# A scan's inputs, shifted through a scratch buffer in memory instead of 32 small on-chip transfers

## The chip, the core and the metric

The kernel runs on one core of a Trainium2 chip. TensorE (PE in the profile) multiplies, its weight loads are listed as PEld; VectorE (DVE), ScalarE (ACT) and GpSimd (POOL) do the rest; SyncE (SP) issues nearly all transfers, in its own order, one after the other. The metric is the device time of one execution in microseconds (us).

## The reference

One layer of an encoder trunk on 256 tokens of width 2048, in float32. A normalised input goes through one projection whose columns feed three groups, each normalised, joined and projected back; then an MLP of width 8192 follows.

```python
h = rmsnorm(x, norm_mix_pre[l])
proj = h @ w_in[l]
q_na, k_na, v_na, u_ssm, q_mem = jnp.split(proj, ...)
y_na = neighbourhood_attention(...)          # 8 heads of 128
y_ssm = s5_mixer(u_ssm, ...)                 # 32 groups of 16 channels, 64 complex states each, both directions
y_mem = memory_cross_attention(q_mem, ...)   # 4 heads, 256 memory tokens
y = jnp.concatenate([rmsnorm(y_na, ...), rmsnorm(y_ssm, ...), rmsnorm(y_mem, ...)], axis=-1)
x = x + rmsnorm(y @ w_out[l], norm_mix_post[l])
f = jnp.square(jax.nn.relu(rmsnorm(x, norm_mlp_pre[l]) @ w_ff1[l])) @ w_ff2[l]
x = x + rmsnorm(f, norm_mlp_post[l])
```

The `s5_mixer` is a linear recurrence over the tokens. Its input `u_ssm` (512 channels) is multiplied into the states (the increments), a scan runs over them forward and backward, and the states are multiplied out again.

## The kernel before

**Weights.** All weight matrices come as one stream of chunks of 128 x 1024 values (512 KB) in the order in which they are used (`plan`). `w_dma` issues chunk after chunk on SP into three raw buffers (`wraw`); a chunk may only be issued when VectorE has done with the chunk three before it. ACT copies a chunk into a rounded high part (`wh`), VectorE subtracts to get the low part (`wl`), and each product is three matmuls: high x high, high x low, low x high. `take(n)` hands the next n column blocks to TensorE; at the start of a chunk it has the chunk two ahead converted, and at its start and its middle it calls `tick`.

**Side work.** Everything that is not a weight matmul is a generator with a priority (a smaller number goes first), started by `spawn`. `tick` runs those that are due, by a planner's clock for each engine (`clk`, with costs written in the kernel); `after(ns)` lets that much of the planner's TensorE time go by, `until(f)` waits for a condition, and `drain` runs one to its end. The planner sets only the order in which instructions are written down for each engine. On the chip each engine takes its own list in order and waits at each instruction for what it needs.

**The scan.** The first 16 chunks give the mixer's input in `big`, and `g0_evac` writes it to `uT`: 128 partitions x 4 tiles (`ut`) x 256 tokens. The token order is such that a group's four consecutive tokens lie in four stretches of 64 columns. The increments want these four side by side in the partitions: `U4`, 128 x 16 x 64. 32 transfers of 16 partitions x 4 x 64 values move it there, all issued in a row on SP. `prep_b` makes the input weights of a tile in four power steps (`W`) on VectorE, has TensorE turn them, copies them to `W1T` and spawns `incr`, which multiplies them with `U4` as soon as `ssm_done` says that it is there by the plan, 6000 ns after the last issue. A tile has two increments (forward, backward) of 16 matmuls of 64 x 64; the profile lists each as two records. ACT puts the results in `XS`; `tree` scans two tiles at a time on VectorE (`ps`, `XS`), `ssm_out` multiplies out, and what follows prepares `yH`, `yL` for the gate's matmuls.

**The heads.** In the third stage (two groups of four heads) `att_task` does one head of the neighbourhood attention with priority 1, in six or so steps across the engines. `na_fin` then splits each head's result into `mixn`, high on ACT and low on VectorE, and the output projection's first group uses the heads in their order, two to a chunk.

The mixer's and the memory attention's stage lies around 60 to 130 us in the profile, the heads' after it to about 308 us, the output projection to about 425 us, the MLP behind that.

Of the kernel before, what the change touches and what calls it, by code (L numbers as in the profile page):

```python
# [11 lines left out]
F32 = mybir.dt.float32  # L12
# [19 lines left out]
NB = S // 4  # L32
# [11 lines left out]
SH_G = 500.0  # L44
BACK_V, BACK_G, BACK_A, BACK_TREE = 2600.0, 4000.0, 3000.0, 1700.0
WARM0, WARM1 = 7, 10
SUM_LAG = 5000.0
LAM_BACK = 900.0
GLU_AT = 2
# [55 lines left out]
def hybrid_kernel(ctx: ExitStack, tc: tile.TileContext, A: dict, out: bass.AP, dbg=None):  # L105
    nc = tc.nc
# [52 lines left out]
    V, G, ACT, PE = (Engine(e, r) for e, r in zip("VGAE", (nc.vector, nc.gpsimd, nc.scalar, nc.tensor)))  # L159
# [2 lines left out]
    wpool = ctx.enter_context(tc.tile_pool(name="wpool", bufs=3))  # L162
    small = ctx.enter_context(tc.tile_pool(name="small", bufs=4))
    ps = ctx.enter_context(tc.tile_pool(name="ps", bufs=1, space=PSUM))

    def acc():
        return ps.tile([128, 512], F32, name="acc", tag="bank", bufs=6)

    def att():
        return ps.tile([128, 512], F32, name="att", tag="bank", bufs=6)  # L170
# [4 lines left out]
    def tt(eng, o, a, b, op):  # L175
        eng.tensor_tensor(o, a, b, op=op)
# [10 lines left out]
    def act(o, i, f=AF.Copy, **kw):  # L187
        ACT.activation(o, i, f, **kw)
# [38 lines left out]
    def col(base, i=0):  # L227
        return vecs[:, base + i:base + i + 1]
# [7 lines left out]
    def spawn(gen, pri=1, uses="VA", after=None):  # L236
        i = sum(1 for t in tasks if t[0] <= pri)
        tasks.insert(i, [pri, gen, clk[after] + MARGIN + LAG[min(pri, 2)] if after else clk["E"], uses])
        return gen
# [37 lines left out]
    def after(ns):  # L277
        t = clk["E"] + ns
        while clk["E"] < t:
            yield  # L280

    def wait_for(g):
        while live(g):
            yield

    def done(e):

        t = clk[e] + MARGIN
        while clk["E"] < t:
            yield  # L290
# [152 lines left out]
    a2 = A2.enter_context(tc.tile_pool(name="a2", bufs=1, side="right"))  # L443
# [215 lines left out]
    uT = a2.tile([128, 4, 256], F32, name="uT")  # L659
    U4 = a2.tile([128, 16, NB], F32, name="U4")  # L660
# [9 lines left out]
    def prep_b(ut):  # L670
        yield from until(lambda: ut in loaded and clk["E"] > loaded[ut][1])
        raw = loaded[ut][0]

        wf = a2.tile([128, WROW], F32, name="W", tag="W", bufs=1)

        def power(l):
            a, n = (3 - l) * 16, WSTEP + (2 * l - 3) * 16
            return (wf[:, a:a + 2 * n].rearrange("p (d x) -> p d x", d=2)[:, :, 0:512]
                    .rearrange("p d (n l b) -> p d n l b", n=8, l=4)[:, :, :, 0, :])

        par = a2.tile([128, 4, 2, 2, 4], F32, name="par", tag="par", bufs=1)
        for i, x in enumerate((cfr, cfi, lbr, lbi)):
            act(par[:, i], x[:, 8 * ut:8 * ut + 8].rearrange("p (d q) -> p d q", d=2)[:, :, None, :]
                .to_broadcast([128, 2, 2, 4]))
        yield from done("A")
        for l in range(4):
            o = power(l)
            src = power(l - 1) if l else raw.rearrange("p (d n b) -> p d n b", d=2, n=8)
            r_, i_ = (par[:, 2 * min(l, 1) + i].rearrange("p d c q -> p d (c q)")[:, :, :, None]
                      .to_broadcast([128, 2, 8, 16]) for i in range(2))  # L690
            t = a2.tile([128, 2, 8, 16], F32, name="pt", tag="pt", bufs=1)
            tt(V, t, src, i_, mult)
            tt(V, o, src, r_, mult)
            tt(V, o[:, :, 0:4], o[:, :, 0:4], t[:, :, 4:8], sub)
            tt(V, o[:, :, 4:8], o[:, :, 4:8], t[:, :, 0:4], add)
            yield True
        yield from done("V")
        for d in range(2):
            act(W0[ut][:, d].rearrange("p c q j b -> p (c q) j b"),
                power(0)[:, d][:, :, None, :].to_broadcast([128, 8, 2, 16]))  # L700
        w0_done.add(ut)
        if ut % 2 == 0:
            XS[ut // 2] = a2.tile([128, 2, 16, NB], F32, name="XS", tag="AB", bufs=2)
        yield from done("A")
        for d in range(2):

            wt = a2.tile([128, 2, 4, 64], F32, name="W1T", tag="W1T", bufs=2)
            p = att()
            for n in range(8):
                for j in range(2):  # L710
                    h = slice(64 * j, 64 * j + 64)
                    PE.matmul(p[h, 64 * n:64 * n + 64], wf[h, WSTEP * d + 64 * n:WSTEP * d + 64 * n + 64], ident[h, h],
                              start=True, stop=True, skip_group_check=True, tile_position=(64 * j, 64 * j))
            act(wt.rearrange("p c q m -> p (c q m)"), p)
            spawn(incr(ut, d, wt, clk["A"] + MARGIN + LAG[2]), 2, "A")
            yield True
# [131 lines left out]
    ssm_done = []  # L848

    prepc, k0s, trees, out_done, w0_done, xs_part = (set() for _ in range(6))  # L850
    lam_done, pw_done, den_done = [], [], []

    def until(f):
        while not f():
            yield
# [125 lines left out]

    drain(rx)

    def g0_evac():
        b = st_rx["b"]
        for j in range(2):
            tt(V, qkm[:, 2 * j:2 * j + 2, 0, :], pq[j].rearrange("p (a b) -> p a b", a=2),
               b[:, None, :].to_broadcast([128, 2, 256]), mult)
        yield
        for u in range(4):  # L990
            tt(V, uT[:, u].rearrange("p (r c) -> p c r", c=16),
               pu[:, u * 256:(u + 1) * 256].rearrange("p (c r) -> p c r", c=16), b.rearrange("p (c r) -> p c r", c=16),
               mult)
        yield

        for q in range(4):
            for j in range(2):
                for i in range(4):
                    r = 64 * j + 16 * i
                    nc.sync.dma_start(U4[r:r + 16, q:16:4, :],  # L1000
                                      uT[32 * q + 16 * j:32 * q + 16 * j + 16, :, i * NB:(i + 1) * NB])
        yield from after(6000.0)
        ssm_done.append(1)
        if dbg:
            dbg("uT", uT.rearrange("p a b -> p (a b)"))
        yield
# [47 lines left out]
    def mem_task():  # L1054
        for h in range(MEMH):
            yield from att_task(qkm[:, h], vm[:, :, h * 128:(h + 1) * 128], None, (mixm[:, 0, h, :], mixm[:, 1, h, :]),
                                "mo", col(V_MO, h))
        yield from after(SUM_LAG)
        st_rx["mo"], _ = yield from rms([sums["mo"]], 1.0 / 512, "mo", bcast=False)
# [7 lines left out]
    def load_bias(h):  # L1067
        biasT[h] = a1.tile([128, 2, WIN_K], F32, name="bias", tag="xst", bufs=2)
        nc.sync.dma_start(biasT[h], A["bias"][h])

    for g in range(2):
        pv2 = [acc(), acc()]
        for k in range(KT):
            wh, wl = take(4)
            for t in range(2):
                s = slice(t * 128, (t + 1) * 128)
                mm_tok(pv2[t], xH[:, k, s], xL[:, k, s], wh, wl, start=(k == 0), stop=(k == KT - 1))
        vt = a1.tile([128, 2, 512], F32, name="v", tag="v", bufs=2)
        for t in range(2):
            act(vt[:, t, :], pv2[t], AF.Copy, scale=rsX[:, t:t + 1])  # L1080
        for h in range(4 * g, 4 * g + 4):
            load_bias(h)
            pp = acc()
            for j in range(2):
                for k in range(KT):

                    no_tree[0] = j == 1 and k >= KT - CH
                    wh, wl = take(1)
                    mm3(pp[:, j * 256:(j + 1) * 256], wh, wl, xH[:, k, :], xL[:, k, :], start=(k == 0),
                        stop=(k == KT - 1))  # L1090
            no_tree[0] = False
            qk = a1.tile([128, 2, 256], F32, name="qk", tag="qk", bufs=2)
            tt(V, qk, pp.rearrange("p (a b) -> p a b", a=2), rbX[:, None, :].to_broadcast([128, 2, 256]), mult)
            hh = h % 4
            naT.append(spawn(att_task(qk, vt[:, :, hh * 128:(hh + 1) * 128], biasT[h], yna[:, h, :], "na", None),
                             pri=1, after="V"))
    drain(mt)


# [11 lines left out]
    def na_rms():  # L1111
        yield from wait_for(nf)
        yield from after(SUM_LAG)
        st_rx["na"], _ = yield from rms([sums["na"]], 1.0 / 1024, "na", bcast=False)
# [130 lines left out]
    for t, c, _ in parts:  # L1245
        p = acc()
        s = slice(t * 128, (t + 1) * 128)
        b = slice(c.start - 1536, c.stop - 1536)
# [121 lines left out]
    def x1_task():  # L1370
        for o in range(4):
            for t in range(2):
# [8 lines left out]
    rt, r22, r24, vb, v, y, tn, r = (small.tile([128, 2], F32, name=n, bufs=1)  # L1381
                                 for n in ("rt2", "r22", "r24", "vb", "fv", "fy", "ft", "fr2"))
# [28 lines left out]
    for half in range(2):  # L1411
# [19 lines left out]
        for o in range(4):  # L1431
# [26 lines left out]
            if o < 3:  # L1458
                for t in range(2):
                    if half == 0:  # L1460
                        act(facc[:, t, c], po[t])
                    else:
                        tt(V, facc[:, t, c], po[t], facc[:, t, c], add)
                        q = cp.tile([128, 512], F32, name="ff", tag="ff", bufs=2)
# [88 lines left out]
```

## Time and profile before

| | |
|---|---|
| median of three runs | 1147.5 us (1146.65 to 1147.84) |
| profiled execution, its own time | 1145.56 us |
| its span, first to last instruction | 1143.8 us |
| instructions | 18188 |
| TensorE's mean granted clock | 0.991 |

In the profile's rows the first numbers are the start in us and the duration in us; then engine, line, operation, output tile and input tiles, shapes and count. In square brackets stands how long the engine was idle before and what ended that. Since every operation goes through one helper, nearly all rows carry its line, 156; tiles tell the groups apart. The row of a transfer on SP (`SPq`) is its issue, not its travel; "to landing" is from issue to the data's arrival. A row with x2 or more merges neighbours of one kind, and a matmul's modelled end overlaps the next one's start, so the distance of starts is the time that it takes.

### The profile page before, as it was taken

What the parts mean: (1) busy time and instruction counts of PE and PEld (TensorE: products, weight loads), DVE (VectorE), ACT (ScalarE), POOL (GpSimd) and SP (SyncE); (2) the same over time, 40 slices, a digit from 0 to 9 for tenths busy, and PEclk for the clock granted to TensorE, in tenths of its full rate; (3) what the DMA queues carried; (4) which work ended last, traced back from release to release, by engine and by line L of the source; (5) the groups of instructions that cost most, each with busy time, mean ns of one, the idle gap of its engine ahead of it and who ended that gap; (6) DMA issues with size and microseconds to landing.
All of it is one profiled execution on the core that took longest, in us unless ns stands there. A gap on an engine that the chain in (4) does not pass through costs nothing.

```text
span 1143.8 us, 18188 instructions
## 1 busy us (share of the span) xinstructions
PE 1113.1 (97%) x7144; PEld 962.5 (84%) x7144; DVE 717.4 (63%) x1068; ACT 563.6 (49%) x872; POOL 103.1 (9%) x171
## 2 busy tenths in 40 slices
PE   8996999999999999999999999999999999999996
PEld 8985889989977878888888888888888888888885
DVE  6783798899756766766665444445666665445454
ACT  6653665566564474544545434434544544344341
POOL 1760000020010061000000000000000000001010
PEclk9998999999999999999999999999999999999998
DMA  8873454445545665666666666666666665666673
GB/s 301 300 214 110 152 164 146 150 141 166 166 148 165 217 218 174 187 193 191 187 191 189 188 185 188 189 191 186 189 194 188 188 194 188 185 197 195 195 209 126
DMA packets 65287, 212.85 MB, mean 186 GB/s; under 512 B 9776, under 2 KB 12336, under 8 KB 65200
## 3 DMA queue, kind: packets, MB, share of 16 engines
q1 hardware_dynamic: 64912, 211.58, 60.5%
q8 instruction: 56, 0.92, 0.3%
q14 instruction: 31, 0.25, 0.1%
q10 hardware_dynamic: 288, 0.09, 0.0%
HBM read 209.02 MB, written 2.10 MB: 185 GB/s over the span
## 4 chain that ended last, share of the span: by engine, by line
PE 86%; DMA 3%; DVE 3%; POOL 3%; issue 2%; SPq 1%; ACT 1%; DVEq 0%; POOLq 0%; ACTq 0%
PE acc L156 77%; PE big L156 5%; PE att L156 5%; DMA wraw<-in_w_dram 3%; SPq L1000 1%; DVE wl L156 1%; ACT wh L156 1%; POOL u L156 1%; DVE W L156 0%; POOL cs L156 0%; POOL x L156 0%; DMA gpost<-in_post_dram 0%; POOL q L156 0%; POOL t L156 0%; POOL acc L156 0%
## 5 line engine op out<-in xcount | busy, mean ns | idle before, releaser
L156 DVE TENSOR_TENSOR wl<-wraw,wh 128x1024 fp32r<-128x1024 f32 (+1 forms) x372 | 458.9, 1235 | 378.7 <-ACT wh L156 378.3
L156 ACT ACTIVATE wh<-wraw 128x1024 fp32r<-128x1024 f32 (+1 forms) x372 | 391.5, 1054 | 456.4 <-PE acc L156 236.8
L156 PE MATMUL acc<-hs,wh 128*128 128x512 f32 (+1 forms) x996 | 346.0, 391 | 0.0
L156 PE MATMUL acc<-hs,wl 128*128 128x256 f32 x992 | 279.6, 282 | 0.0
L156 PEld LDWEIGHTS acc<-hs,wh 128*128 128x128 f32 x996 | 186.6, 188 | 38.4 <-ACT hs L156 0.2
L156 PEld LDWEIGHTS acc<-hs,wl 128*128 128x128 f32 x992 | 187.7, 189 | 0.0
L156 PE MATMUL acc<-wh,fH 128*128 128x512 f32 x448 | 178.9, 399 | 0.0
L156 PE MATMUL acc<-wh,fL 128*128 128x512 f32 x448 | 176.7, 394 | 0.0
L156 PE MATMUL acc<-wl,fH 128*128 128x512 f32 x448 | 175.7, 392 | 0.0
L156 PEld LDWEIGHTS acc<-wh,fL 128*128 128x128 f32 x448 | 84.1, 188 | 21.9
L156 PEld LDWEIGHTS acc<-wl,fH 128*128 128x128 f32 x448 | 84.2, 188 | 20.0
L156 PEld LDWEIGHTS acc<-wh,fH 128*128 128x128 f32 x448 | 84.1, 188 | 19.2
L156 PE MATMUL acc<-xH,wh 128*128 128x256 f32 x256 | 74.5, 291 | 0.0
L156 PE MATMUL acc<-xH,wl 128*128 128x256 f32 x256 | 71.9, 281 | 0.0
L156 PE MATMUL acc<-xL,wh 128*128 128x256 f32 x256 | 71.9, 281 | 0.0
L156 POOL TENSOR_TENSOR facc<-facc,g 128x512 f32<-128x512 f32 x6 | 9.6, 1622 | 476.5 <-DMA g<-in_g_dram 476.5
L156 PEld LDWEIGHTS acc<-xH,wh 128*128 128x128 f32 x256 | 48.4, 189 | 0.7
L156 PEld LDWEIGHTS acc<-xL,wh 128*128 128x128 f32 x256 | 48.4, 189 | 0.1
L156 PEld LDWEIGHTS acc<-xH,wl 128*128 128x128 f32 x256 | 48.3, 189 | 0.0
L156 PE MATMUL acc<-wh,mixn 128*128 128x512 f32 x128 | 41.5, 399 | 2.6 <-DVE half L156 1.4
L156 DVE TENSOR_TENSOR ps<-XS,pw 128x32 f32<-128x32 f32 (+9 forms) x44 | 30.3, 689 | 2.4 <-ACT XS L156 0.9
L156 PEld LDWEIGHTS acc<-wh,mixn 128*128 128x128 f32 x128 | 23.9, 188 | 8.8 <-DVE half L156 1.8
(303 smaller groups left out, 1452.1 us busy)
## 6 DMA issues: line engine op xcount, KB each, us to landing
wraw<-in_w_dram SPq DMA_DIRECT2D x369, 512.0 KB, 3.6
tokst<-in_xt_dram SPq DMA_DIRECT2D x4, 512.0 KB, 7.7
mst<-in_memT_dram SPq DMA_DIRECT2D x4, 512.0 KB, 5.0
tokst<-in_mt_dram SPq DMA_DIRECT2D x4, 512.0 KB, 5.9
x<-in_xt_dram SPq DMA_DIRECT2D x8, 256.0 KB, 5.6
out_dram<-facc SPq DMA_DIRECT2D x8, 256.0 KB, 2.5
xst<-in_xT_dram SPq DMA_DIRECT2D x7, 256.0 KB, 6.6
bias<-in_bias_dram SPq DMA_DIRECT2D x8, 160.0 KB, 3.8
```

The costliest lines, as they stand in the source:

```text
L156: return f(o, *a, **kw)
L1000: nc.sync.dma_start(U4[r:r + 16, q:16:4, :], uT[32 * q + 16 * j:32 * q + 16 * j + 16, :, i * NB:(i + 1) * NB])
```

## The change

The shift now goes through a scratch tensor `ud` in the chip's memory. Eight transfers write to it, each from 16 partitions, 64 KB in 256 pieces of 64 values; one transfer of 128 x 1024 values reads it back into `U4`. The eight are no longer issued in a row, but by a side task `shift` of priority 2, which lets 1300 ns of planned time pass after each. The increments are let in 14000 ns of planned time after the fetch is written down. Since turned weights wait longer for their use, `W1T` has four buffers, and a tile's weights are only turned when the tile two before it has its increments. The last two heads' attention gets priority 0.

```diff
+SHIFT_LAG = 14000.0
...
+    dram = ctx.enter_context(tc.tile_pool(name="dram", bufs=1, space=bass.MemoryType.DRAM))
...
         yield from done("A")
+        yield from until(lambda: ut < 2 or (ut - 2, 1) in xs_part)
         for d in range(2):
 
-            wt = a2.tile([128, 2, 4, 64], F32, name="W1T", tag="W1T", bufs=2)
+            wt = a2.tile([128, 2, 4, 64], F32, name="W1T", tag="W1T", bufs=4)
...
+    def shift():
+
+        ud = dram.tile([128, 16, NB], F32, name="ud")
+        for q in range(4):
+            for j in range(2):
+                r = 32 * q + 16 * j
+                nc.sync.dma_start(ud[64 * j:64 * j + 64, q:16:4, :].rearrange("(i b) u n -> b u i n", i=4),
+                                  uT[r:r + 16].rearrange("p u (i n) -> p u i n", i=4))
+                yield from after(1300.0)
+        nc.sync.dma_start(U4, ud)
+        yield from after(SHIFT_LAG)
+        ssm_done.append(1)
+
     def g0_evac():
...
-
-        for q in range(4):
-            for j in range(2):
-                for i in range(4):
-                    r = 64 * j + 16 * i
-                    nc.sync.dma_start(U4[r:r + 16, q:16:4, :],
-                                      uT[32 * q + 16 * j:32 * q + 16 * j + 16, :, i * NB:(i + 1) * NB])
-        yield from after(6000.0)
-        ssm_done.append(1)
+        spawn(shift(), 2, "V")
...
             naT.append(spawn(att_task(qk, vt[:, :, hh * 128:(hh + 1) * 128], biasT[h], yna[:, h, :], "na", None),
-                             pri=1, after="V"))
+                             pri=1 if h < 6 else 0, after="V"))
```

The SP queue in the memory attention's stage, before (`wraw` is a weight chunk, `U` the shifted input, `mst` and `Cw` other inputs):

```order
L459 DMA mst<-in_memT_dram 128x1024
L320 DMA wraw<-in_w_dram 128x1024
L1000 DMA U_112<-uT 16x4x64 x32
L320 DMA wraw<-in_w_dram 128x1024 x4
L741 DMA Cw<-in_c_dram 128x256
```

and after the change, whose lines are two or so further down:

```order
L461 DMA mst<-in_memT_dram 128x1024
L322 DMA wraw<-in_w_dram 128x1024 x2
L993 DMA ud<-uT 64x4x64
L322 DMA wraw<-in_w_dram 128x1024
...
L744 DMA Cw<-in_c_dram 128x256
L322 DMA wraw<-in_w_dram 128x1024 x3
L993 DMA ud<-uT 64x4x64
L322 DMA wraw<-in_w_dram 128x1024
...
L993 DMA ud<-uT 64x4x64
L322 DMA wraw<-in_w_dram 128x1024
L996 DMA U_114<-ud 128x1024
```

The 32 issues between two weight chunks are gone; eight stand singly, each behind one chunk, and the fetch one chunk behind the last of them.

TensorE at the first tile's increments, before, in the memory attention's stage (`memS` is its split input):

```order
L156 MATMUL acc<-memS,wh 128x256 x2
L156 MATMUL acc<-memS,wl 128x256
L156 MATMUL att<-U_112,W1T 64x64 x32
L156 MATMUL acc<-wh,memS 128x512
L156 MATMUL acc<-wl,memS 128x512
```

and after the change, ten of sixteen steps into the following matrix (`xH`, `xL` are the split main input):

```order
L157 MATMUL acc<-wl,xH 128x512
L157 MATMUL acc<-wh,xL 128x512
L157 MATMUL att<-U_114,W1T 64x64 x64
L157 MATMUL att<-CC,W_240 32x96 x16
L157 MATMUL acc<-wh,xH 128x512
```

The increments of the first two tiles now stand together, at the start of the fifth weight chunk behind the one with the fetch; the first tile's are 174 weight matmuls further back, the second's 42.

VectorE where the last heads are split, before (`wl` is a weight chunk's low part, `U` a step of the mixer's end):

```order
L156 SCALAR_TENSOR_TENSOR mixn<-yna,vecs,mixn 128x256
L156 TENSOR_TENSOR wl<-wraw,wh 128x1024 x2
L156 SCALAR_TENSOR_TENSOR mixn<-yna,vecs,mixn 128x256 x2
L156 TENSOR_TENSOR wl<-wraw,wh 128x1024
L156 SCALAR_TENSOR_TENSOR U_112<-gt,uT 128x16x16
L156 SCALAR_TENSOR_TENSOR mixn<-yna,vecs,mixn 128x256
```

and after the change:

```order
L157 TENSOR_TENSOR wl<-wraw,wh 128x1024 x2
L157 SCALAR_TENSOR_TENSOR mixn<-yna,vecs,mixn 128x256
L157 TENSOR_TENSOR wl<-wraw,wh 128x1024
L157 SCALAR_TENSOR_TENSOR U_114<-gt,uT 128x16x16
L157 TENSOR_TENSOR wl<-wraw,wh 128x1024
L157 SCALAR_TENSOR_TENSOR mixn<-yna,vecs,mixn 128x256
L157 MEMSET half 128x1
L157 TENSOR_TENSOR wl<-wraw,wh 128x1024
L157 SCALAR_TENSOR_TENSOR mixn<-yna,vecs,mixn 128x256
```

The first `mixn` row of the change is head 5's, then heads 6 and 7: head 5's has moved two weight splits forward, head 7's stays behind the same split, and the `U` step is no longer between that split and it.

## The prediction

> **What bounds the kernel now.** I read the page first (busy shares and the chain that ended last), then the busy time by stretches, and then the engines' own rows in the one stretch that stands out.
>
> ```profile
> PE 1113.1 (97%) x7144; PEld 962.5 (84%) x7144; DVE 717.4 (63%) x1068; ACT 563.6 (49%) x872; POOL 103.1 (9%) x171
> PE 86%; DMA 3%; DVE 3%; POOL 3%; issue 2%; SPq 1%; ACT 1%; DVEq 0%; POOLq 0%; ACTq 0%
> ```
>
> TensorE is busy for 97% of the span, and the chain runs through it for 86%. So a change that takes no matmul away can only win what TensorE loses, and the busy time by stretches says where that is. The columns are the stretch, its length, busy time of PE, weight loads, DVE, ACT and POOL, the granted TensorE clock, the DMA engines' share and GB/s:
>
> ```profile
> 68.00:88.50 20.50, 19.41 (x165) 17.55 (x165) 18.04 (x35) 10.77 (x21) 10.30 (x21) 0.92 0.55 160
> 88.50:103.40 14.90, 5.02 (x67) 4.16 (x65) 0.00 (x0) 0.32 (x1) 0.00 (x0) 0.67 0.31 84
> 103.40:130.00 26.60, 25.85 (x201) 22.23 (x200) 22.75 (x56) 18.71 (x27) 0.18 (x1) 0.99 0.53 168
> 130.00:200.00 70.00, 70.00 (x777) 64.26 (x777) 58.78 (x104) 41.99 (x90) 0.85 (x2) 1.00 0.49 150
> 250.00:308.00 58.00, 58.00 (x640) 56.62 (x642) 54.05 (x96) 35.94 (x71) 5.44 (x9) 1.00 0.59 175
> 308.00:345.00 37.00, 35.61 (x320) 28.95 (x309) 16.76 (x22) 22.32 (x41) 4.48 (x6) 1.00 0.47 140
> 345.00:400.00 55.00, 53.50 (x257) 43.88 (x256) 38.59 (x71) 25.02 (x35) 2.22 (x3) 1.00 0.62 191
> ```
>
> From 88.5 to 103.4 us TensorE works for 5.02 of 14.90 us, DVE and ACT for nothing or nearly so, at a clock of 0.67. Two later stretches lose 1.4 and 1.5 us; 130 to 200 and 250 to 308 lose none. The timeline of TensorE and of the SP queue shows the big loss:
>
> ```profile
> 88.49 0.28 PE L156 MATMUL acc<-memS,wl 128*128 128x256 f32 x1
> 88.70 0.44 PE L156 MATMUL att<-U,W1T 64*64 64x64 f32 x6
> 90.29 0.30 PE L156 MATMUL att<-U,W1T 64*64 64x64 f32 x2 [1.16 <-DMA U<-uT]
> ...
> 100.50 3.00 PE L156 MATMUL att<-U,W1T 64*64 64x64 f32 x50 [2.01 <-DMA U<-uT]
> 103.43 0.60 PE L156 MATMUL acc<-wh,memS 128*128 128x512 f32 x1
> ```
>
> ```profile
> 77.24 0.33 SPq L320 DMA_DIRECT2D wraw<-in_w_dram  x1
> 77.63 21.48 SPq L1000 DMA_DIRECT2D U<-uT  x32
> 99.22 6.54 SPq L320 DMA_DIRECT2D wraw<-in_w_dram  x4
> ```
>
> ```profile
> ACT wh L156 <- DMA wraw<-in_w_dram: 24.1, 5, 15.9
> ```
>
> The 32 shift transfers hold the SP queue for 21.48 us (0.67 us each). The first 64 increment records wait for them inside TensorE's order, and the weight chunks wait behind them: the last row, of the waits between 66 and 130 us, has ACT's copy waiting 15.9 us for one. Either wait alone would stop TensorE here, so both must go.
>
> **Part 1: the shift leaves the critical stretch.** From 88.70 to 103.43 TensorE spends 14.73 us on 64 increment records. The same work with its inputs there:
>
> ```profile
> 130.11 2.08 PE L156 MATMUL att<-U,W1T 64*64 64x64 f32 x64
> 132.12 0.91 PE L156 MATMUL att<-CC,W 128*32 128x96 f32 x32
> 79.34 0.40 PE L156 MATMUL acc<-memS,wh 128*128 128x256 f32 x2
> 82.16 0.40 PE L156 MATMUL acc<-memS,wh 128*128 128x256 f32 x2
> ```
>
> 132.12 - 130.11 = 2.01 us, so the stretch loses 14.73 - 2.01 = **12.72 us**. The last two rows start two neighbouring weight chunks: one chunk is 2.82 us of TensorE. It is 12 matmuls of 256 columns and 6 of 512, so 0.235 us for a wide one and 0.118 for a narrow one. In the changed order the increments of the first two tiles stand five chunks (14.1 us) behind the fetch of the shifted inputs, so they need it to land within that; the 2.01 us of each tile's matmuls is paid later and is already in the sum.
>
> What takes the place of the 32 issues? Eight, one behind each of eight weight chunks, and one fetch. Rows for what an issue costs and how a chunk and a shift transfer land:
>
> ```profile
> L1000 SPq DMA_DIRECT2D U<-uT x32: 585/593/970, 77.6 to 98.5; - x32
> DMA to landing us min/median/max: 1.8/1.9/5.3
> L320 SPq DMA_DIRECT2D wraw<-in_w_dram x372: 327/328/713, 1.2 to 1117.9; - x186
> DMA to landing us min/median/max: 2.5/3.6/8.8
> SPq L320 <- DVE wl L156: 29.9, 12, 4.7
> q1 hardware_dynamic: 1840, 0.38, 13.3%
> ```
>
> The trace has no issue of 256 pieces. From below it is a plain transfer's 0.33 us, from above four times the old one's 0.59 us for 64 pieces, 2.36 us; I take 0.97, the longest of the 32, since 128 pieces of a weight chunk cost no more than 0.33. Cover: a chunk comes every 2.82 us and its own issue takes 0.39 (77.24 to 77.63), so SP has 2.43 us per chunk, in which it now waits for VectorE (29.9 us in 12 waits between 66 and 136 us). Even 2.36 us fits under it, so I cost the eight at **0**; without that cover they would be 8 x 0.97 = 7.8 us. Queued behind each is only the next weight chunk, which ACT reads; its slack is what counts. For the DMA engines: between 84 and 99 us 1840 packets, nearly all of the old transfers, took 13.3% of 16 engines over 15 us, 31.9 us or 17.3 ns each. The outs move the same 2048 pieces: 35.5 us over 16 engines is 2.2 us, and the fetch is a chunk's worth, against a DMA share of 0.53. Also 0.
>
> [...] The pieces are 256 B and now go to memory, not to the on-chip buffer; no run so far shows such a write. [...]
>
> **Part 2: a wait that came with it.** After the burst of weight chunks VectorE is late once more:
>
> ```profile
> 104.17 1.23 DVE L156 TENSOR_TENSOR wl<-wraw,wh 128x1024 fp32r<-128x1024 f32 x1 [16.44 <-ACT wh L156]
> 113.52 0.56 PE L156 MATMUL acc<-memS,wh 128*128 128x256 f32 x2
> 114.83 0.38 PE L156 MATMUL acc<-memS,wl 128*128 128x256 f32 x1 [0.75 <-DVE wl L156]
> ```
>
> Two of these narrow matmuls take 0.24 us, so the third was due at 113.76 and lost 1.07. It comes from the split at 104.17 starting 0.74 us after TensorE resumed in mid-chunk (half a chunk is 1.41), that is 2.15 us into the chunk. Without the stall that split follows ACT's copy (1.06 us) at about 1.2 us, one us better. Bounds 0 and 1.07; I take **0.7**, as the power steps behind it stay in VectorE's list.
>
> **Part 3: the last heads.** In the first output group TensorE waits twice for attention heads:
>
> ```profile
> 341.83 0.40 PE L156 MATMUL acc<-wl,mixn 128*128 128x512 f32 x1
> 343.22 0.74 PE L156 MATMUL acc<-wh,mixn 128*128 128x512 f32 x2 [0.99 <-DVE mixn L156]
> 345.89 0.40 PE L156 MATMUL acc<-wl,mixn 128*128 128x512 f32 x1
> 347.65 0.73 PE L156 MATMUL acc<-wh,mixn 128*128 128x512 f32 x2 [1.36 <-DVE half L156]
> 344.47 1.06 ACT L156 ACTIVATE wh<-wraw 128x1024 fp32r<-128x1024 f32 x1 [1.85 <-PE acc L156]
> 345.56 1.23 DVE L156 TENSOR_TENSOR wl<-wraw,wh 128x1024 fp32r<-128x1024 f32 x1 [2.00 <-ACT wh L156]
> 346.70 0.58 DVE L156 SCALAR_TENSOR_TENSOR U<-gt,uT 128x256 f32<-128x256 f32 x1
> 347.13 0.46 DVE L156 SCALAR_TENSOR_TENSOR mixn<-yna,vecs,mixn 128x256 fp32r<-128x256 f32 x1
> ```
>
> At 0.235 us per matmul they were due at 342.07 and 346.12: 1.15 us are lost at head 5 and 1.53 at head 7. In the changed order head 5's low half stands two weight splits earlier, so its 1.15 goes. Head 7's keeps its place behind a weight split that can't start before TensorE has left the chunk before (ACT 344.47, DVE 345.56); only the `U` step ahead of it leaves, 347.13 - 346.70 = 0.43. So **1.58**, and 1.10 stays; bounds 0 (the heads are late elsewhere) and 2.68 (both go).
>
> **Part 4: the four buffers and the later scan.** Two more small buffers and one wait in the planner add no instruction. The scan over the increments starts four chunks later in VectorE's list: 4 x (2.82 - 1.22) = 6.4 us of it are pushed back. VectorE is idle for 11.2 us between 130 and 200, and for 3.95 between 250 and 308, which covers it if it spreads; the second scan ends behind the same weight split as before. Bounds 0 and 6.4; I allow **+0.6** for some wait.
>
> **Sum.** -12.72 - 0.7 - 1.58 + 0.6 = -14.4. The profiled execution took 1145.56 us (span 1143.8 and 1.76 around it), so a profiled one should take 1131.2; it lies 1.9 below the median shown, 1147.5, from which the predicted median is **1133.1 us**.
>
> **Rivals.** *A, slower: the SP queue becomes the stop.* If one of the eight issues holds SP for d us, the next chunk is late by d - 2.43, eight times. It eats the whole gain at d = 2.43 + 14.4/8 = 4.2 us; at 5 us it adds 20.6, 1153.7. For it: four times the pieces, four dimensions. Against it: nothing in the 32 rows goes above 0.97.
>
> *B: the way through memory is slow.* The fetch may only be issued when the last out has landed, and SP stands there with the next chunk behind it. The last out goes one chunk earlier, so beyond a landing of 2.82 + 2.43 - 0.33 = 4.9 us chunks are late. At the weights' worst, 8.8 us, that is 3.9 us: 1137.0. Against it: 1.9 us median for the old ones; for it: 5.3 as their worst. [...]
>
> *C: VectorE crowds.* If the 6.4 us fall where it has only 3.95 idle, TensorE waits 2.5 us for weight splits; if none is covered, 6.4. That is 1135 to 1139.5. For it: 54.05 of 58 us busy; against it: no TensorE loss there now.
>
> *D: the wait only moves*, to the increments' new place, because the fetch lands later than 14.1 us: then most of 12.72 comes back and the time is within 0.2% of 1147.5 or up to 1145.
>
> **How the numbers follow.** Forecast 0.72 (its own range 1130.5 to 1136), C 0.12, B 0.09, D 0.03, A 0.04. The low end is all upper bounds, 12.72 + 1.07 + 2.68 = 16.5, so 1131.0, less 0.5 for the spread of the runs; the high end is C's 1139.5, which holds B too. A measurement here can't tell less than 0.2% (2.3 us) from no change. Forecast, B and C are faster, and most of D: 0.94; same 0.02; slower is A, 0.04.
>
> **What would show it.** Right: no increment record waits for a transfer; the stretch from 88 us on shows TensorE busy and the clock at 1.00; SP's shift issues stand singly between weight chunks, under 2.4 us each; the matmul of head 5 follows without a wait, that of head 7 still waits about 1 us. Wrong: ACT's copies waiting for weight chunks between 80 and 120 us (A or B), weight matmuls waiting for VectorE's splits between 130 and 310 (C), increments waiting for the fetch (D).

## The result, and the profile after

| | before | after |
|---|---|---|
| median of 4 runs each (us) | 1147.08 (1146.43 to 1147.84) | 1131.14 (1130.65 to 1131.40) |
| profiled execution / its span (us) | 1145.56 / 1143.8 | 1131.40 / 1129.6 |
| mean granted TensorE clock | 0.991 | 0.996 |

The ratio is 0.986, 95% interval 0.9843 to 0.9877: 15.9 us less by the medians, 14.2 us less by the two profiled executions. 1133.1 us was predicted, with 1130.5 to 1139.5 as the range.

The page of the changed kernel, its busy shares and the chain that ended last:

```profile
PE 1109.0 (98%) x7144; PEld 958.8 (85%) x7144; DVE 716.3 (63%) x1068; ACT 563.7 (50%) x872; POOL 102.5 (9%) x171
PE 87%; DVE 4%; POOL 3%; DMA 2%; issue 2%; ACT 2%; SPq 0%; DVEq 0%; POOLq 0%; ACTq 0%
```

The SP queue is gone from the chain (0%, before 1%). Busy time by stretches in the changed kernel (stretch, its length, busy PE, weight loads, DVE, ACT, POOL, granted clock, DMA share, GB/s):

```profile
88.50:103.40 14.90, 14.64 (x95) 13.12 (x94) 13.87 (x39) 8.91 (x13) 0.00 (x0) 1.00 0.52 146
115.00:185.00 70.00, 70.00 (x804) 64.63 (x805) 52.72 (x94) 41.02 (x87) 0.18 (x1) 1.00 0.50 153
185.00:292.00 107.00, 105.10 (x1058) 98.15 (x1057) 96.52 (x157) 60.91 (x125) 12.01 (x16) 1.00 0.51 153
330.00:385.00 55.00, 53.69 (x258) 44.19 (x258) 39.43 (x72) 25.13 (x35) 2.22 (x3) 1.00 0.65 197
```

In the first of these stretches TensorE is now busy for 14.64 of 14.90 us at full clock (before: 5.02 us at 0.67). In the third it loses 1.90 us, where the kernel before lost nothing. The SP queue's timeline shows what stands in place of the 21.48 us of issues, and the groups of the scratch tile what an out costs:

```profile
79.08 0.69 SPq L993 DMA_DIRECT2D ud<-uT  x1
82.81 0.33 SPq L322 DMA_DIRECT2D wraw<-in_w_dram  x1
83.19 0.59 SPq L993 DMA_DIRECT2D ud<-uT  x1
...
112.84 0.33 SPq L322 DMA_DIRECT2D wraw<-in_w_dram  x1
113.83 0.33 SPq L996 DMA_DIRECT2D U<-ud  x1
```

```profile
L993 SPq DMA_DIRECT2D ud<-uT x8: 581/586/1172, 79.1 to 110.2; - x8
L996 SPq DMA_DIRECT2D U<-ud x1: 331/331/331, 113.8 to 113.8; - x1
DMA to landing us min/median/max: 3.6/4.6/6.1
```

The outs stand singly between weight chunks, 0.59 us each (median), and land after 3.6 us or more (median 4.5; the last row also counts the fetch). TensorE's timeline after the change, with the first increments, all that it still waits for between 75 and 400 us, and the rows just ahead of two of these waits:

```profile
98.09 0.40 PE L157 MATMUL acc<-memS,wh 128*128 128x256 f32 x2
98.75 0.38 PE L157 MATMUL acc<-memS,wl 128*128 128x256 f32 x1 [0.26 <-DVE wl L157]
...
125.70 3.95 PE L157 MATMUL att<-U,W1T 64*64 64x64 f32 x128
...
204.89 0.50 PE L157 MATMUL acc<-wl,xH 128*128 128x512 f32 x1 [0.44 <-DVE wl L157]
215.35 1.97 PE L157 MATMUL att<-XS,CC 128*32 128x63 f32 x128 [0.56 <-DVE XS L157]
240.74 0.38 PE L157 MATMUL acc<-xH,wl 128*128 128x256 f32 x1 [0.90 <-DVE Cw L157]
...
332.87 0.39 PE L157 MATMUL acc<-wl,mixn 128*128 128x512 f32 x1
334.57 0.73 PE L157 MATMUL acc<-wh,mixn 128*128 128x512 f32 x2 [1.31 <-DVE mixn L157]
```

The 128 increment records of the first two tiles run without a wait. What is left is VectorE: a wait of 0.26 us where the kernel before had one of 0.75 (at 114.83), three new waits of 1.90 us together between 200 and 245, and 1.31 at head 7. Head 5's wait is gone. ACT's copies still wait for weight chunks between 80 and 120 us, 6.5 us in four waits, the longest 1.9; none of that reaches TensorE.

A wait in brackets counts from the modelled end of the matmul before, and so shows less than is lost: by the distance of starts, the prediction's measure, the 0.26 are 98.75 - (98.09 + 0.24) = 0.42 us (before: 1.07) and the 1.31 are 334.57 - (332.87 + 0.235) = 1.47 us (before: 1.53). Both measures are used below, each under its name.

### The profile page after: what moved, and what is told of

Its sections match the earlier page's. It is cut to its first block, busy times and chain, and to the rows that moved or that the text cites. A ratio compares the mean times of both kernels' runs of the same rounds, so it can differ in the third digit from the quotient of the medians.

```text
span 1129.6 us, 18148 instructions
## 1 busy us (share of the span) xinstructions
PE 1109.0 (98%) x7144; PEld 958.8 (85%) x7144; DVE 716.3 (63%) x1068; ACT 563.7 (50%) x872; POOL 102.5 (9%) x171
## 3 DMA queue, kind: packets, MB, share of 16 engines
q1 hardware_dynamic: 64672, 212.10, 62.1%
## 4 chain that ended last, share of the span: by engine, by line
PE 87%; DVE 4%; POOL 3%; DMA 2%; issue 2%; ACT 2%; SPq 0%; DVEq 0%; POOLq 0%; ACTq 0%
PE acc L157 78%; PE big L157 5%; PE att L157 5%; DMA wraw<-in_w_dram 2%; DVE wl L157 2%; ACT wh L157 1%; POOL u L157 1%; DVE W L157 0%; POOL t L157 0%; POOL cs L157 0%; POOL x L157 0%; POOL q L157 0%; DVE pt L157 0%; DVE XS L157 0%; POOL k L157 0%
## 5 line engine op out<-in xcount | busy, mean ns | idle before, releaser
L157 ACT ACTIVATE P<-P,mn 128x160 f32<-128x160 f32 (+1 forms) x24 | 10.8, 449 | 43.9 <-DVE mn L157 43.9
```

The lines of the kernel that those rows point to most:

```text
L157: return f(o, *a, **kw)
```

## Experiments

Each ratio is against the kernel before, run on the same chip beside it (median there 1146.59 us for the first four experiments, 1147.20 for the next four, 1147.06 for the last two). The scheduler makes its lists anew for every edit, so for each experiment it is said whose VectorE list it has: where two kernels have the same list, row for row, they differ in the transfers, the increments' place and a few rows of ACT around them alone. No run takes the four buffers or the wait in the planner away by itself. In the code cuts, lines in brackets or in plain words are notes, and the making of a scratch tensor is left out.

### 1. The heads alone

```diff
 (kernel before)
-                             pri=1, after="V"))
+                             pri=1 if h < 6 else 0, after="V"))
```

> The kernel before with one edit: the last two attention heads run in the scheduler's first class. My theory: the wait of TensorE for head 5 (1.15 us) goes and that for head 7 falls from 1.53 to 1.10 us, so the time is 1.58 us shorter than before, about 1145.5 us, and the loss from 88.5 to 103.4 us stays whole. Rival: the heads' order costs nothing or is worth nothing by itself, because the wait of head 7 takes over what head 5 gives up: within 0.3 us of before. In the changed kernel the first output group waits 1.31 us for head 7 and not for head 5, so by it I expect 1.15 + 0.2 = 1.4 us.

Measured: 1143.64 us, ratio 0.9973 (0.9963 to 0.9983), 2.95 us less. That is more than either expectation (1.58 and 1.4 us); by the interval it is 1.9 to 4.2. Its stretch around the last heads, columns as above:

```profile
330.00:385.00 55.00, 55.00 (x400) 45.90 (x400) 35.26 (x57) 28.44 (x41) 3.55 (x6) 1.00 0.58 172
```

TensorE loses nothing there (before: 2.35 us of waits, 2.68 by starts). In this list head 7's mixing, too, stands one weight split earlier; in the list of the changed kernel, with the same head order, it does not. So the wait of head 7 that I read off the changed order belongs to that order, not to the head edit.

### 2. The burst kept, the increments late

```diff
 (changed kernel: lag, guard, four buffers, head order)
 def shift():
+    32 transfers U4[r:r+16, q:16:4, :] <- uT[...], as before, in one burst
-    eight outs to ud, one per after(1300.0); then U4 <- ud
     yield from after(SHIFT_LAG)
```

> The changed kernel's lag, guard, four buffers and head order, but the shift itself as before: 32 on-chip transfers issued in one burst, no scratch in memory. The increments stand later in TensorE's order, so they no longer wait; the weight chunks still queue behind 21.5 us of issues. My theory (either wait alone stops TensorE): the chunk that is issued at 99.2 us lands, is copied and split by about 103.9, while TensorE runs out of split weights at 90.1 (half a chunk behind 88.7) or, with one more chunk ready, 92.9 us; 11.0 to 13.8 us are lost in place of 12.72, and with the heads' 1.4 the time is 1143 to 1147 us. Rival (the increments' wait was the loss and the weights would have come in time): most of 12.7 us is won, about 1133 us.

Measured: 1148.49 us, ratio 1.0016 (1.0008 to 1.0025): nothing is won, and the 1143 to 1147 us expected are missed. The timelines of the SP queue and of TensorE in this run, and the stretch behind the wait, columns as above:

```profile
80.77 21.54 SPq L992 DMA_DIRECT2D U<-uT  x32
102.41 1.48 SPq L321 DMA_DIRECT2D wraw<-in_w_dram  x3
```

```profile
107.55 0.80 PE L157 MATMUL acc<-memS,wh 128*128 128x256 f32 x2 [11.24 <-ACT wh L157]
108.81 0.58 PE L157 MATMUL acc<-memS,wl 128*128 128x256 f32 x1 [0.46 <-DVE wl L157]
```

```profile
103.40:115.00 11.60, 6.99 (x77) 6.36 (x78) 7.05 (x22) 4.57 (x7) 0.00 (x0) 0.53 0.68 216
```

No increment waits for a transfer any more, and TensorE stands still for 11.24 + 0.46 = 11.70 us all the same, now for a weight chunk. So the weights' wait alone is enough, as the prediction had it (11.0 to 13.8 expected). The other half, that the increments' wait would be enough with the weights in time, has no run. The stop cost more than its length here: the granted clock behind it was 0.53, so that the 6.99 us of busy time hold another 3.3 us of loss, an estimate from these two numbers (6.99 x 0.47; before, the clock from 103.4 to 130 us was 0.99). This is one reason why the time is not below that of before, as expected; the other is shared by the next run.

### 3. The outs in a row

```diff
 (changed kernel)
                 nc.sync.dma_start(ud[...], uT[...])
-                yield from after(1300.0)
         nc.sync.dma_start(U4, ud)
```

> The changed kernel with its eight outs and the fetch issued in a row behind one weight chunk, not spaced; the increments then stand about five chunks earlier in TensorE's order. My theory: SP is held 8 x 0.59 + 4.5 (landing of the last out) + 0.33 = 9.5 us, the next weight chunk is 7.1 us late; from the kernel before, 5.3 to 8.1 us of that are slack of the weights on their way to TensorE, so 0 to 1.8 us are lost between 80 and 100 us, and the earlier scan takes away some of the 1.9 us of waits between 200 and 250 us: 1129.5 to 1133 us. Rival (the bound of 4.9 us that I used for a wait on SP): 9.5 - 4.9 = 4.6 us lost, about 1135.7 us. Rival (the stretch has far more slack): nothing lost, 1129.5 us or less.

Measured: 1136.77 us, ratio 0.9911 (0.9897 to 0.9924). My range, 1129.5 to 1133, is missed. The number is near that of the first rival, but the profile is not that rival's. The SP queue's timeline, and then TensorE's waits for VectorE, all that it has between 75 and 345 us:

```profile
80.45 6.09 SPq L993 DMA_DIRECT2D ud<-uT  x8
88.67 0.35 SPq L995 DMA_DIRECT2D U<-ud  x1
89.07 1.37 SPq L322 DMA_DIRECT2D wraw<-in_w_dram  x3
```

```profile
248.42 0.39 PE L157 MATMUL acc<-xH,wl 128*128 128x256 f32 x1 [0.70 <-DVE wl L157]
252.29 0.39 PE L157 MATMUL acc<-xH,wl 128*128 128x256 f32 x1 [0.80 <-DVE wl L157]
268.95 0.39 PE L157 MATMUL acc<-xH,wl 128*128 128x256 f32 x1 [0.24 <-DVE wl L157]
282.87 0.81 PE L157 MATMUL att<-qk 128*128 128x160 f32 x4 [0.93 <-DVE qk L157]
...
334.85 0.74 PE L157 MATMUL acc<-wh,mixn 128*128 128x512 f32 x2 [0.94 <-DVE mixn L157]
338.86 0.74 PE L157 MATMUL acc<-wh,mixn 128*128 128x512 f32 x2 [0.94 <-DVE mixn L157]
```

SP is held from 80.45 to 89.02 us, 8.57 us, and TensorE does not wait once between 75 and 248 us. The weights have that much slack. Runs 2 and 3 size it. In the changed kernel the chunk behind the first out goes out 3.73 us after it (82.81 - 79.08). By that measure the next chunk went out 17.9 us late in run 2 (102.41 - 80.77 - 3.73), and TensorE waited 11.7, so some 6.2 us are slack, an estimate from this one execution; in run 3 it was 4.9 us late (89.07 - 80.45 - 3.73), which is less. The two runs have the same VectorE list, and even the same order on TensorE and ACT; only the transfers differ. Their medians differ by 1148.49 - 1136.77 = 11.72 us and their profiled executions by 14.09, where run 2's wait and clock make 11.70 + 3.3 = 15.0 us and a pause of 1.34 us in run 3's profile (see run 10) works the other way. That the medians' 11.72 equals the wait alone is chance: run 2's times spread over 3.9 us.

What run 3 loses, it loses between 248 and 340 us, six waits for VectorE of 4.55 us in all, and so does run 2. Run 3's increments:

```profile
97.34 2.08 PE L157 MATMUL att<-U,W1T 64*64 64x64 f32 x64
```

They come 28 us earlier than in the changed kernel (125.70), the scan follows them, and VectorE's list meets TensorE's worse; that the earlier scan is the reason is not shown.

### 4. The 32 transfers on chip, spread

```diff
 (changed kernel; no scratch)
+    32 transfers U4[r:r+16, q:16:4, :] <- uT[...], as before,
+    behind two of every three: yield from after(700.0)
-    eight outs to ud, one per after(1300.0); then U4 <- ud
-SHIFT_LAG = 14000.0
+SHIFT_LAG = 6000.0
```

> The shift as before, 32 on-chip transfers without a scratch in memory, but spread over about 15 weight chunks, one to three behind each; lag 6000, guard, four buffers and head order as in the changed kernel. My theory (what counts is that no weight chunk queues behind more than the 2.43 us that SP has left per chunk): three issues of 0.6 to 0.7 us are at most 2.0 us and stay hidden, the time is 1131 us, up to 1.5 us more since the increments come half a chunk or more later than in the changed kernel. Rival (fewer and larger transfers by way of memory are what helps): the 32 issues cost part of their 21.5 us again, 1135 us or more.

Measured: 1128.35 us, ratio 0.9833 (0.9819 to 0.9847), 2.8 us under the changed kernel. The old transfers work as well as the new ones once they are spread; one to three issues between chunks cost TensorE nothing here, where from 75 to 395 us it waits only once, 0.26 us for VectorE. But this kernel's list differs from the changed one's too:

```profile
135.88 3.95 PE L157 MATMUL att<-U,W1T 64*64 64x64 f32 x128
```

The increments come 10 us later than there, so the 2.8 us may be the transfers' or the list's. Run 7 separates that.

### 5 and 6. The old lists, with the shift moved

```diff
 (changed kernel)
                 nc.sync.dma_start(ud[...], uT[...])
-                yield from after(1300.0)
+                if j == 1:
+                    yield from after(1300.0)
 (run 5 only)
-                             pri=1 if h < 6 else 0, after="V"))
+                             pri=1, after="V"))
```

With two outs behind each of four chunks VectorE's list comes out, row for row, as in the kernel before (run 5) and as in run 1 (run 6).

> The changed kernel without the head order and with its eight outs issued two behind each of four weight chunks: by this VectorE's list is the same, row for row, as in the kernel before, and only the shift and the first 64 increments have moved. My theory (the stall of 12.72 us and VectorE's lateness behind it, 0.81, are all that the move takes away): 13.5 us shorter than before, about 1133.3 us, ratio 0.988, with the waits for heads 5 and 7 still there and no new wait between 190 and 310 us. Rival (moving the increments costs something by itself): those waits come with it, 1135 us or more.

> The same with the head order: VectorE's list is then, row for row, that of the run with the heads alone. My theory (the two parts add up, and what the changed kernel gives back between 200 and 340 us comes from the planner's new list and not from the shift): the 2.95 us of the heads and the 13.5 of the move, 16.5 together, about 1130.2 us, no wait of TensorE between 105 and 395 us. Rival (moved increments and early heads get into each other's way whatever the list is): the 1.9 us of waits between 200 and 245 us and the 1.3 us at head 7 are there again, 1132 us or more.

Measured: run 5 1130.70 us, ratio 0.9861 (0.9847 to 0.9874), 16.5 us less than before; run 6 1126.55 us, ratio 0.9821 (0.9808 to 0.9835), 20.65 us less. Run 6 beats both kernels. The stretches of run 6, columns as above, and then TensorE's waits for heads in run 5:

```profile
185.00:292.00 107.00, 107.00 (x1093) 100.49 (x1095) 96.17 (x152) 61.89 (x125) 14.44 (x18) 1.00 0.52 160
292.00:330.00 38.00, 38.00 (x440) 31.58 (x429) 20.46 (x27) 23.19 (x42) 4.59 (x6) 1.00 0.48 144
330.00:385.00 55.00, 55.00 (x265) 45.54 (x264) 38.22 (x69) 27.30 (x39) 4.54 (x5) 1.00 0.67 211
```

```profile
328.21 0.73 PE L157 MATMUL acc<-wh,mixn 128*128 128x512 f32 x2 [0.99 <-DVE mixn L157]
332.63 0.73 PE L157 MATMUL acc<-wh,mixn 128*128 128x512 f32 x2 [1.35 <-DVE half L157]
```

Run 6 has TensorE busy without a gap from 185 to 385 us; run 5 has the two waits for heads of before, 0.99 and 1.35 us, and none between 190 and 310. Run 5's gain of 16.5 us (14.5 to 17.6 by the interval) is above the 13.5 expected; the two profiled executions differ by 15.6. The starts of the same matmuls tell where: run 5 is 0.79 us ahead of the kernel before at 73.26 us (74.05 there), 14.65 ahead at 117.47 (132.12), so 13.9 us belong to the moved shift, near the 13.5; the sections on run 10 and on the clock show where differences of the other kind come from. Moving the shift brings no wait of its own, then, and the head order is worth what it was worth alone (4.15 us by these medians, 2.64 by the two profiled executions, 2.95 in run 1). Run 6 is 3.7 us below the 1130.2 expected, for the same reason: it gains 15.0 us on run 1 between 73.47 and 117.29 us (73.83 and 132.68 there), since run 1's stall is a longer one, and run 1 has a pause besides (see run 10). The changed kernel has both edits and misses 4.6 us of run 6. Between the two lie the list and the pairing of the outs, and run 7 shows that the way by memory costs nothing against the one on chip.

### 7. The changed kernel, a longer lag

```diff
-SHIFT_LAG = 14000.0
+SHIFT_LAG = 20000.0
```

> The changed kernel with a lag of 20000 in place of 14000: VectorE's list is then, row for row, that of the run with 32 spread on-chip transfers, and the two differ only in how the inputs are shifted, eight outs and a fetch by way of memory or 32 transfers on chip. My theory (the way of the transfers costs nothing as long as no chunk queues behind them): the same time as that run, 1128.4 within 0.5 us, about 2.5 us under the changed kernel. Rival (the way by memory costs the difference that those two showed): about 1131 us.

Measured: 1128.32 us, ratio 0.9838 (0.9824 to 0.9851), against 0.9833 in run 4. Two ways of shifting, one list, one time. By this list TensorE has, between 100 and 395 us, no wait for VectorE, only 0.30 us put down to "issue". The lag is one number; 6 us more of it are worth 2.8 us.

### 8. The changed kernel without the head order

```diff
-                             pri=1 if h < 6 else 0, after="V"))
+                             pri=1, after="V"))
```

> The changed kernel with the last two heads in their old class. My theory: TensorE waits for heads 5 and 7 as before, 2.35 us in the view of its waits against 1.31 in the changed kernel, so 1.0 to 1.4 us longer, 1132.1 to 1132.5 us. Rival (the order is worth here what it was worth alone): 2.95 us, about 1134 us. Rival (it is worth nothing, since the planner makes another list anyway): 1131 us.

Measured: 1131.18 us, ratio 0.9862 (0.9849 to 0.9876). It is the time of the changed kernel: my theory, 1.0 to 1.4 us more, is wrong, the last rival right. TensorE's waits in this run, in the stretch with the heads:

```profile
331.81 0.73 PE L157 MATMUL acc<-wh,mixn 128*128 128x512 f32 x2 [0.94 <-DVE mixn L157]
346.02 0.39 PE L157 MATMUL acc<-yL,wh 128*128 128x256 f32 x1 [0.90 <-DVE yL L157]
```

In this list only head 7's matmul waits even without the edit. The edit takes away the second wait, for `yL`, and makes head 7's longer: 0.94 + 0.90 = 1.84 us of waits against 1.31 in the changed kernel. The 0.5 us between them do not show in the medians.

### 9. The outs doubled

```diff
                 nc.sync.dma_start(ud[...], uT[...])
+                nc.sync.dma_start(ue[...], uT[...])
                 yield from after(1300.0)
```

> The changed kernel with each of the eight outs issued twice, the second time to a second scratch that nothing reads; every engine's list but SP's is the same. My theory (an issue of 0.59 us is covered by the 2.43 us that SP has left per chunk, and the weights have some 7 us of slack besides): 1.2 us per chunk are covered too, the time of the changed kernel, 1131.1 within 0.6 us, landing of an out 4 to 5 us. Rival (each out costs what it holds SP, 0.59 us): 4.7 us more, about 1135.8 us. Rival (pieces of 256 bytes written to memory are the slow part, so that twice as many land much later and the fetch, which SP waits for, holds up the next chunk): landing above 8 us and 1133 us or more.

Measured: 1131.40 us, ratio 0.9867 (0.9851 to 0.9884), the changed kernel's time within 0.3 us; its outs land after 4.5 us (median), the second ones after 3.9. The 4.7 us of the first rival would be clear of the spread, and no out lands after more than 5.9 us, where the second rival had 8. An issue of an out between weight chunks cost no time that shows here, and neither did twice as many (1131.40 against 1131.14 us).

### 10. The kernel before, once more

> The kernel before, unchanged, profiled once more. Its first profile was of an execution 1.5 us under the median of its runs, and the move of the shift alone has shortened the medians by 16.5 us where stall and late split add up to 13.5. My theory: this execution shows the same stall within 0.5 us (12.7) and the same waits of TensorE, and a difference in time from the first goes with stretches at a lower granted clock outside the stall, of some 1.5 us each. Rival (the stall varies from execution to execution and is longer in the slower ones): 64 increments that take 16 us or more.

Measured: one execution, 1149.56 us, 4.0 us above the first profiled one. TensorE's timeline with the first and last of the increments and a pause that the first profile did not have, the SP queue's timeline, and the stretch around the pause:

```profile
88.63 0.45 PE L156 MATMUL att<-U,W1T 64*64 64x64 f32 x6
...
104.33 0.50 PE L156 MATMUL acc<-wh,memS 128*128 128x512 f32 x1
...
311.53 0.39 PE L156 MATMUL acc<-wl,mixm 128*128 128x512 f32 x1 [1.73 <-issue]
```

```profile
77.57 22.49 SPq L1000 DMA_DIRECT2D U<-uT  x32
```

```profile
310.00:320.00 10.00, 8.47 (x36) 7.16 (x35) 1.39 (x4) 4.17 (x10) 0.00 (x0) 0.83 0.14 49
```

The stall took 104.33 - 88.63 = 15.70 us (14.73 in the first), as the burst held SP for 22.49 us (21.48); at 311.53 TensorE paused for 1.73 us, and in the ten microseconds around it the clock was 0.83, another 1.7 us by estimate (10 x 0.17; TensorE was busy for 8.47 of them, so at least 1.4). 0.97 + 1.73 + 1.7 = 4.4 us, against the 4.0 to be explained. Both theories were half right: stall and clock vary. Run 1's stall is of the longer kind (88.11 to 103.85 us, SP held for 22.46). What the pause put down to "issue" is, stays open; it stands at 1.46 us in run 1, 1.34 in run 3, and under 0.4 us in the other profiles.

## Why the prediction was right, and where not

- **Part 1, the stall (12.72 us).** Right, with one claim untested. The weights' wait alone stops TensorE (run 2: 11.70 us, and no such wait once SP's hold is shorter, run 3); that the increments' wait alone would do so was argued from their rows and has no run. The eight issues cost nothing (run 9); the increments find their inputs (no wait in any kernel that moved them). The size was a little low: two more profiles with the burst show 15.70 and 15.74 us where the first had 14.73. And what wins is the spreading, not the way by memory: 32 spread transfers on chip do as well (runs 4 and 7).
- **An issue of 256 pieces, taken at 0.97 us within 0.33 to 2.36.** It took 0.59 (median 0.586), no more than one of 64 (0.593). Nothing hung on it.
- **Part 2, VectorE's lateness (0.7 of 1.07).** Right: by starts 1.07 became 0.42, so 0.65. (The expectations of runs 5 and 6 took 0.81, the 1.07 by starts less the 0.26 of the bracket.)
- **Part 3, the heads (1.58).** The step that failed is "head 5's low half stands two weight splits earlier, so its 1.15 goes": true of the changed list (head 5's wait goes; head 7's is 1.47 by starts, I had 1.10), but it is not the head edit that does it. With that edit alone 2.95 us go, both waits whole (run 1); without it the changed kernel is as long as with it (run 8). I had compared two finished lists and booked their difference to one of three edits that had made them.
- **Part 4, the later scan (0.6 allowed).** Mis-sized: three waits of 1.90 us between 200 and 245, 2.8 us by starts (table below). And it is not that the scan is later: in run 7 it comes later still and nothing is lost; in runs 2 and 3 it comes earlier and 4.55 us of waits stand there. What counts is how a list happens to fit, and why one fits and another does not stays open; the idle time of VectorE, from which I took my bounds, doesn't tell that.
- **The sum.** -14.4 was forecast for a profiled execution, 1131.2; it took 1131.4. That agreement is partly luck. The starts of the same matmul in the two profiles show how the 14.16 us came about:

  | matmul, start before / after (us) | ahead (us) | gained since | forecast |
  |---|---|---|---|
  | `memS,wl` ahead of the first increments, 88.49 / 88.12 | 0.37 | 0.37 | nothing |
  | `CC,W` behind the second tile's, 143.81 / 129.58 | 14.23 | 13.86 | 13.42 (Parts 1 and 2) |
  | `xH,wl`, 204.43 / 190.22 | 14.21 | -0.02 | |
  | `xH,wl`, 264.74 / 253.29 | 11.45 | -2.76 | -0.6 (Part 4) |
  | `wl,mixn` ahead of head 5, 341.83 / 330.07 | 11.76 | 0.31 | nothing |
  | `yH,wl` behind the heads, 362.05 / 348.54 | 13.51 | 1.75 | 1.58 (Part 3) |
  | the end | 14.16 | 0.65 | nothing |

  Part 4 was 2.2 us too small. Part 1 was too small the other way (13.86 - 0.65 = 13.2 for 12.72), and 1.3 us in three places that no part speaks of made up for most of the rest. (Part 3's stretch also holds 0.41 us of a wait for `yL` that the kernel before had.)
- **From the profiled execution to the median.** This step failed and makes the 2.0 us between 1133.1 and 1131.14. I carried over that the profiled execution lay 1.9 us under the median. It was a short execution of the kernel before (run 10: stall 1 us shorter, no pause, one dip of the clock fewer), and the changed kernel has no such stall to vary; its profiled execution lies 0.26 over its median.
- **The rivals.** A fell: two outs per chunk were free (runs 5, 6, 9), and even 8.57 us in one piece cost no wait (run 3). B fell with its bound: 4.9 us left out the slack that the weights have on their way to TensorE, some 6.2 us; landing did rise from 1.9 to 4.5 us, SP stood 0.5 us for the last out, and TensorE did not wait. C came true as a mechanism: its sign, weight matmuls that wait for VectorE between 130 and 310, is there, and 2.8 us by starts is the low end of its 2.5 to 6.4; the time stayed under its 1135 because the median was set 2.0 us too high and by the gains that no part speaks of. D fell: the increments came at 125.70 us, 11.9 behind the fetch's issue at 113.83 and not 14.1; the fetch landed 6.1 us after its issue, and nothing waited.

## What to carry to other kernels

A queue that carries a stream of weights should not get a burst that is longer than the slack of that stream (here 3.7 us until the next chunk is due and, by the estimate of run 3's section, some 6.2 that it may be late; 8.57 us cost no wait, 21.5 cost 11.7). Spread between chunks, the transfers cost no time that shows here, whichever way they went (1128.35 us on chip, 1128.32 by memory, runs 4 and 7). Where a scheduler writes the order, every edit gets a new list, and lists that differ by a lag or a pairing alone differed here by up to 10 us (runs 3 and 6) with no transfer waited for by TensorE in either: hold the list fixed to price an edit, and then search over the lag, which cost one number and brought 2.8 us, or over the pairing, which brought 4.6. And one profiled execution's distance from its median is not a constant to carry over to another kernel.

## What the runs showed of the hardware

**Small pieces to memory.** An out of 256 pieces of 256 bytes held SP no longer than an on-chip transfer of 64 such pieces (0.586 against 0.593 us), but landed after 4.5 us in place of 1.9, with four times the pieces. The DMA queue's packets in stretches that hold small ones alone, first for the outs in a row (run 3, 85.5 to 88.5 us), then for the on-chip burst of run 2 (90 to 101 us); columns are packets, MB, and share of 16 engines:

```profile
q1 hardware_dynamic: 1455, 0.35, 62.1%
```

```profile
q1 hardware_dynamic: 1360, 0.28, 13.3%
```

62.1% of 16 engines for 3 us is 29.8 us, 20.5 ns a packet; 13.3% for 11 us is 23.4 us, 17.2 ns. Most of that difference is the mix: in the burst a fifth of the packets (272) have 4 bytes and take 9 ns, in the outs 95. The 256-byte pieces alone took 20.2 ns on average in run 3 (all 2048 of them) and 19.2 in the burst, with a median of 18 in both. So by these records a small piece written to memory took hardly longer here than one moved on chip, 20.2 against 19.2 ns.

**The clock after a short wait.** In every profile TensorE waits 1.6 to 2.4 us in two steps around 68 us. In seven of the twelve the clock then falls (mean 0.72 from 69 to 75 us), in five not (1.00), though the lists are the same up to there; first the kernel before, then run 5:

```profile
70.00:72.00 2.00, 2.00 (x11) 2.00 (x10) 2.00 (x5) 0.88 (x1) 1.75 (x7) 0.50 0.80 205
72.00:74.00 2.00, 2.00 (x9) 1.62 (x9) 2.00 (x3) 0.68 (x3) 1.92 (x3) 0.76 0.52 100
```

```profile
70.00:72.00 2.00, 2.00 (x15) 1.81 (x14) 2.00 (x6) 1.36 (x2) 1.76 (x8) 1.00 0.64 172
72.00:74.00 2.00, 1.73 (x13) 1.45 (x12) 2.00 (x3) 0.80 (x2) 1.92 (x3) 1.00 0.26 96
```

At 0.50 and 0.76 for 2 us each the kernel before loses 2 x 0.50 + 2 x 0.24 = 1.5 us that run 5 keeps (less the 0.27 us of its own wait there), an estimate from these rows; the starts agree, since a wide matmul takes 0.43 us there at 71.76 us and 0.24 at 75.12, back at 1.00. So in this execution the waits cost their length and, with the fall of the clock behind them, some 1.5 us more; this is part of the 15.6 us between these two profiles (1145.56 and 1129.97) that the moved shift, with its 13.9, does not explain. The length of the waits does not decide alone whether the clock falls: in the kernel before it fell behind waits of 1.17 and 0.81 us, in run 7 behind 0.74 and 0.81, and in run 6 it stayed at 1.00 behind the longer ones of 1.62 and 0.81. What decides it is not shown.
